# Earlier weights for the third input tile, convolved rows split by token chunk, and a final scale worked out in quarters, in a two-layer hybrid encoder

## The chip, the cores and the metric

The kernel runs on one core of a Trainium2 chip. The metric is the device time of one launch in microseconds (us), as a median over runs. Five engines work side by side, each through its own list of instructions in order: TensorE (PE; its weight loads are shown apart as PEld), VectorE (DVE), ScalarE (ACT), GpSimd (POOL) and SyncE (SP), which issues most of the DMAs.

## The reference

Sixteen learned tokens are put ahead of 1024 input tokens (1040 in all, width 1024), two layers follow, then a norm. Cut to what matters here:

```python
for l in range(DEPTH):                       # DEPTH = 2
    h = h + hybrid_mixer(rmsnorm(h, norm1_w[l]), ...)
    h = h + swiglu(rmsnorm(h, norm2_w[l]), w_gate_up[l], w_down[l])
h = rmsnorm(h, final_norm_w)                 # over the 1024 features of a token
return h[:, N_META:]

def hybrid_mixer(h, ...):
    proj = h @ w_in
    qkv = silu(depthwise_conv_centred(qkv, conv_qkv_w))      # conv over 3 tokens
    o = chunk_gated_delta_rule(forward) + flip(chunk_gated_delta_rule(backward))
    o = o * rsqrt(mean(o * o) + eps) * dn_norm_w * silu(z)
    y_sc = sc_b * depthwise_conv_centred(sc_c * sc_h, sc_conv_w)
    return concatenate([o, y_sc]) @ w_out
```

All of it is float32.

## The kernel before

Features lie on the 128 partitions and tokens along the free axis, so a row tile is 128 features of all 1040 tokens, and the residual is eight such tiles, `hr[0]` to `hr[7]`. A float32 product is made of three matmuls: each operand is split into a high part `hi` (a copy rounded to the matmul's format, made by ACT) and a low part `lo` (the operand less `hi`, made by a subtraction on DVE or POOL); `dense` (L145 to L172) issues hi x hi, hi x lo and lo x hi (L156, L157, L158) for each 128 rows of the contraction, chunk of tokens by chunk of tokens, and then calls the function that empties the PSUM bank. Layer 0 cuts the tokens into three chunks (`FULL`: 348, 346, 346), layer 1's outputs into two of 512 (`TAIL`), and the last down projection of all into 512, 256 and 256 (`FIN`).

**Weights.** `wload` brings 1024 rows of weights in two halves: `wsplit` (L123) issues a DMA on SP to a staging tile `raw` (two of them), ACT makes `whi` (L129), and POOL, or DVE where `lov` says so, makes `wlo` (L130). There are three buffers for `whi` and three for `wlo`. Loads run ahead by way of the dictionary `pre`.

**Input projection.** `seq` gives the order of the first eight tiles, four for the keys and four for the queries. For each: `inproj`, scaling by the token's rstd (L647 for the first tiles, whose products are made before rstd is known), `conv` (one ACT pass, L307, and two DVE passes, L308 and L309), then the call that loads the weights of the next tile, `pre[nxt]`. The first two tiles' weights are loaded ahead of the loop.

**Scan and output projection.** `scan_step(d, c, ...)` handles one chunk of 128 tokens in one direction (L802 to L846): products on PE, DVE's updates of the state, ACT's copies of `vr` (L812 scaled, L814 plain). The short-convolution branch leaves four rows, three of them in DRAM (`yd`), which are read back and split (L899 on ACT; L900 on DVE, row 1's on POOL) into `ys`; the first half of the output projection runs on them under the scan. `finalize` writes the scan's output to `O`, which is split by quarters of the tokens (`hcut`, L928 on ACT, L929 on DVE) for the second half, `out_part`.

**End.** In the last layer the last four feature blocks' products are added to the residual in `FIN` order: per chunk and tile `add_h` (L905, DVE, from PSUM), the square (L187, ACT) and its sum over tiles (L188, DVE), and the scale by the final norm's weight (L1428, ACT). `finish_rstd` (L192) then sums over partitions with a matmul by ones (L196), takes the root on ACT (L197) and the reciprocal over all of the chunk's columns on DVE (L198). DVE and POOL take turns multiplying the tiles (L1432), and SP sends them out in pairs (L1433).

**What sets the order.** The program is written in one order, with priorities: `at_prio` moves a stretch to another place, and `after` adds a wait. The engines' lists are then laid out by a scheduler that simulates the program (`schedule_with_timeline_sim=True`), taking by priority what it believes to be ready. So an edit changes the order through priorities and through the simulated times.

Of the kernel before, what the change touches and what calls it, by code (L numbers as in the profile page):

```python
# [42 lines left out]
def trunk(ctx: ExitStack, tc: tile.TileContext, xT, w_in, w_ba, w_out, w_gu, w_dn,  # L43
# [15 lines left out]
    def row(tag, dt=F32, bufs=1):  # L59
        return sb.tile([128, L], dt, tag=tag, bufs=bufs, name=nm(tag))  # L60
# [218 lines left out]
    for l in range(DEPTH):  # L279
# [357 lines left out]
        for pos, i in enumerate(seq):  # L637
            hh = pos % 4
            if pos == 2:
                gate_weights()  # L640
                evp[0] = base - 60000
            lov[0] = pos > 3
            t = trow()
            late = pos < (2, 1)[l]
            inproj(i, to_row_late(t) if late else to_row(t), pfirst if l == 0 and pos == 1 else None)
            if late:
                tt(out=t, in0=t, in1=rstd, op=ALU.mult)  # L647
            dst = (QT if i < 4 else KTt)[:, hh, :]
            conv(t, dst, P_CV + 3 * i)
            if i >= 4:  # L650
                lengths("k", hh, dst, t)
            if pos == 2:
                g, negG, nGb, negE, gl, bkd = gates()
            nxt = seq[pos + 1] if pos < 7 else 8
            if nxt not in pre:
                pre[nxt] = wload(w_in[l, nxt], KT)
            if pos == 3:
                jobs.append(None)
                jobs.extend([lambda c=c: k_out(c) for c in range(9)])
                jobs2.extend([None, None] + [lambda c=c: chunk_p(c) for c in range(9)])  # L660
# [107 lines left out]
        fin = row(Y[1] + "f")  # L768
        nfin = [0]
        done = set()  # L770

        def v4(t, p=128):
            return t[0:p].rearrange("p (h e) -> p h e", h=4)

        def scan_step(d, c, first, final):
            n = 16 if c == 0 else 128
            s0 = 0 if c == 0 else 16 + 128 * (c - 1)
            base = d * 2048
            V, K, A, Qd = (rec[:, base + 512 * i:base + 512 * i + 512].rearrange("p (h e) -> p h e", h=4) for i in range(4))
            dma(V[0:n].rearrange("p h e -> p (h e)"), vkd[c, 0:n, 0, :])  # L780
            if not final:
                dma(K[0:n].rearrange("p h e -> p (h e)"), vkd[c, 0:n, 1, :])
            if c > 0:
                dma(A.rearrange("p h e -> p (h e)"), aqd[c, d, :, 0, :])
# [12 lines left out]
            if first:  # L797
                r = V
            else:
                ks = b0  # L800
                for h in range(H):
                    mm(ks[0:n, h, :], KTt[:, h, s0:s0 + n], St[d][:, h, :], start=True, stop=True)  # L802
                r = vn
                for h in range(H):
                    stt(out=r[0:n, h, :], in0=ks[0:n, h, :], scalar=negE[0:n, d, c, h:h + 1], in1=V[0:n, h, :], op0=ALU.mult, op1=ALU.add)
            vr = b1
            for h in range(H):
                mm(vr[0:n, h, :], Zs[h], r[0:n, h, :], start=True, stop=True)
            need_o = not (c == 0 and d == 0)
            for h in range(H):  # L810
                if not final:
                    act(out=vs[0:n, h, :], in_=vr[0:n, h, :], func=AF.Copy, scale=bkd[0:n, d, c, h:h + 1])  # L812
            if need_o:
                act(out=vn[0:n], in_=vr[0:n], func=AF.Copy)  # L814
            if not final:
                su = b0
                for h in range(H):
                    mm(su[:, h, :], K[0:n, h, :], vs[0:n, h, :], start=True, stop=True)
            extra = None
            if c == 0 and d == 1:  # L820

                vr2 = b0
                for h in range(H):
                    mm(vr2[0:n, h, :], Z0[0][:, h, :], V[0:n, h, :], start=True, stop=True)
                extra = v4(vv[:, 512:1024])
                act(out=extra[0:n], in_=vr2[0:n], func=AF.Copy)
            if need_o:
                po = b1
                for h in range(H):
                    if not first:  # L830
                        mm(po[0:n, h, :], Qs[h], St[d][:, h, :], start=True, stop=False, skip_group_check=True)
                    mm(po[0:n, h, :], As[h], vn[0:n, h, :], start=first, stop=extra is None, skip_group_check=True)
                    if extra is not None:
                        mm(po[0:n, h, :], at0[0][:, h, :], extra[0:n, h, :], start=False, stop=True, skip_group_check=True)
            if not final:
                for h in range(H):
# [52 lines left out]
        hr = [hb[m // 4][:, m % 4, :] for m in range(KT)]  # L889
        t0 = o0  # L890
        yh = big(X[0][2], F32R)
        ys = []
        for i in range(4):
            t = trow() if i < 2 else hb[1][:, i, :] if i < 3 else y3
            if i < 3:
                dma(t[:, t0:L], yd[i][:, t0:L])
            yl = row(X[1], F32R, 3) if i < 3 else row(X[1] + "f", F32R)
            for (n0, n1) in (chunks if i == 3 else [(t0, L)]):
                act(out=yh[:, i, n0:n1], in_=t[:, n0:n1], func=AF.Copy)  # L899
                (ptt if i == 1 else tt)(out=yl[:, n0:n1], in0=t[:, n0:n1], in1=yh[:, i, n0:n1].bitcast(F32), op=ALU.subtract)  # L900
            ys.append((yh[:, i, :], yl))

        def add_h(m, then=None):
            def f(ps, n0, n1):
# [21 lines left out]
        for (n0, n1) in hcut[0] + hcut[1]:  # L926
            for h in range(H):
                act(out=oh[:, h, n0:n1], in_=O[:, h, n0:n1], func=AF.Copy)  # L928
                tt(out=ol[:, h, n0:n1], in0=O[:, h, n0:n1], in1=oh[:, h, n0:n1].bitcast(F32), op=ALU.subtract)  # L929
        os_ = [(oh[:, h, :], ol[:, h, :]) for h in range(H)]  # L930

        def half(ap, z):
# [485 lines left out]
        if not last:  # L1418
            for m in range(KT):
                then = next_norm(m, x[m], par[:, (l + 1) * P_L + P_N1 + m:(l + 1) * P_L + P_N1 + m + 1], ss)  # L1420
                dense(pre.pop(("dn", m)) if m < 2 else wload(w_dn[l, m, :, 0:NF, :], NF), rest, chunks, add_h(m, then), pwide)
                dma(hd[m], hr[m])
        else:
            for (n0, n1) in FIN:
                for m in range(KT):
                    dense(wds[m], rest, [(n0, n1)], add_h(m), pwide)
                    add_sq(hr[m][:, n0:n1], ss[:, n0:n1], m == 0)
                    act(out=hr[m][:, n0:n1], in_=hr[m][:, n0:n1], func=AF.Copy, scale=par[:, 2 * P_L + m:2 * P_L + m + 1])  # L1428
                finish_rstd(ss, [(n0, n1)])
                for m in range(0, KT, 2):  # L1430
                    for q in (m, m + 1):
                        (tt, ptt)[q % 2](out=hr[q][:, n0:n1], in0=hr[q][:, n0:n1], in1=ss[:, n0:n1], op=ALU.mult)  # L1432
                    dma(out[m:m + 2, :, n0 - 16:n1 - 16].rearrange("m p t -> p m t"), hb[m // 4][:, m % 4:m % 4 + 2, n0:n1])  # L1433
        if not last:
            finish_bc(ss, 0, L, rsd[1])
        hsrc = hd
# [73 lines left out]
```

## Time and profile before

| | us |
|---|---|
| median of 3 runs | 2610.71 |
| lowest and highest | 2609.76, 2611.3 |
| the profiled execution's own time | 2609.5 |
| span of its trace | 2607.7 |

The 1.8 us between the profiled execution's time and its span lie outside the traced instructions. In the profile a row of the timeline gives the start and the duration in us, the engine (a q behind it means its sequencer), the line of the kernel, the operation, what it writes and reads, its shape, how many instructions are merged in the row (x), and in brackets how long the engine had been idle before it and what ended that. `L156` is line 156. Tile names carry no numbers, so `a` and `b` are any tile of those two groups.

### The profile page before, as it was taken

What the parts mean: (1) busy time and instruction counts of PE and PEld (TensorE: products, weight loads), DVE (VectorE), ACT (ScalarE), POOL (GpSimd) and SP (SyncE); (2) the same over time, 40 slices, a digit from 0 to 9 for tenths busy, and PEclk for the clock granted to TensorE, in tenths of its full rate; (3) what the DMA queues carried; (4) which work ended last, traced back from release to release, by engine and by line L of the source; (5) the groups of instructions that cost most, each with busy time, mean ns of one, the idle gap of its engine ahead of it and who ended that gap; (6) DMA issues with size and microseconds to landing.
All of it is one profiled execution on the core that took longest, in us unless ns stands there. A gap on an engine that the chain in (4) does not pass through costs nothing.

```text
span 2607.7 us, 45131 instructions
## 1 busy us (share of the span) xinstructions
PE 2506.3 (96%) x17442; PEld 2291.1 (88%) x17442; DVE 1663.3 (64%) x2481; ACT 1043.8 (40%) x1933; POOL 1113.8 (43%) x838
## 2 busy tenths in 40 slices
PE   8999999999999999999999989999989999999997
PEld 6889999998899999999998978998967778887786
DVE  4678433648766666778455874235687776668756
ACT  5563332435233333444445633224342333333534
POOL 2141212225666666655320202222267766665552
PEclk9999999999999999999999989999999999999998
DMA  3458265524432222664224582545343222238631
GB/s 126 128 181 265 91 207 165 182 67 133 131 98 86 100 81 78 219 211 144 77 95 132 188 275 71 183 158 199 107 126 129 95 93 89 85 107 270 188 98 65
DMA packets 213571, 360.03 MB, mean 138 GB/s; under 512 B 25268, under 2 KB 87676, under 8 KB 213356
## 3 DMA queue, kind: packets, MB, share of 16 engines
q1 hardware_dynamic: 180684, 310.69, 36.6%
q10 hardware_dynamic: 30496, 42.09, 5.2%
q0 software_dynamic: 2176, 4.36, 0.6%
q8 instruction: 137, 2.24, 0.4%
q14 instruction: 78, 0.64, 0.1%
HBM read 266.60 MB, written 90.46 MB: 137 GB/s over the span
## 4 chain that ended last, share of the span: by engine, by line
PE 53%; DVE 9%; DMA 5%; issue 3%; POOL 2%; ACT 1%; SPq 0%; POOLq 0%; DVEq 0%; ACTq 0%
PE pacc L156 4%; PE pacc L158 4%; PE pacc L157 4%; PE pacc L1060 3%; PE pacc L1062 3%; PE pacc L1061 3%; PE pf L1060 2%; PE pb L1060 2%; PE pf L1062 2%; PE pb L1062 2%; PE pb L1061 2%; PE pf L1061 2%; PE pacc L1409 2%; PE pacc L1407 2%; PE pacc L1408 2%
## 5 line engine op out<-in xcount | busy, mean ns | idle before, releaser
L130 POOL TENSOR_TENSOR wlo<-raw,whi 128x512 fp32r<-128x512 f32 x132 | 177.0, 1342 | 789.5 <-ACT whi L129 685.1
L156 PE MATMUL pacc<-a,whi 128*128 128x346 f32 (+1 forms) x808 | 265.2, 331 | 11.7 <-ACT whi L129 8.8
L158 PE MATMUL pacc<-a,wlo 128*128 128x346 f32 (+1 forms) x808 | 264.8, 330 | 2.2 <-DVE wlo L130 1.5
L156 PE MATMUL pacc<-b,whi 128*128 128x346 f32 (+2 forms) x672 | 235.3, 351 | 0.0
L158 PE MATMUL pacc<-b,wlo 128*128 128x346 f32 (+2 forms) x672 | 233.6, 349 | 0.0
L157 PE MATMUL pacc<-a,whi 128*128 128x346 f32 (+1 forms) x688 | 226.4, 329 | 1.8 <-DVE a L900 1.8
L129 ACT ACTIVATE whi<-raw 128x512 fp32r<-128x512 f32 x168 | 105.1, 628 | 243.8 <-PE pacc L157 173.8
L157 PE MATMUL pacc<-b,whi 128*128 128x346 f32 (+2 forms) x580 | 200.6, 347 | 0.5 <-DVE b L900 0.5
L156 PEld LDWEIGHTS pacc<-a,whi 128*128 128x128 f32 x808 | 154.0, 191 | 16.8 <-ACT whi L129 10.4
L1043 POOL TENSOR_TENSOR wlo<-rw,whi 128x512 fp32r<-128x512 f32 x92 | 135.8, 1477 | 72.3 <-ACT whi L1042 70.6
L158 PEld LDWEIGHTS pacc<-a,wlo 128*128 128x128 f32 x808 | 154.4, 191 | 4.1 <-DVE wlo L130 1.9
L156 PEld LDWEIGHTS pacc<-b,whi 128*128 128x128 f32 x672 | 127.6, 190 | 11.0 <-issue 3.1
L157 PEld LDWEIGHTS pacc<-a,whi 128*128 128x128 f32 x688 | 131.4, 191 | 5.8 <-issue 3.4
L158 PEld LDWEIGHTS pacc<-b,wlo 128*128 128x128 f32 x672 | 127.8, 190 | 9.2 <-issue 0.8
L1043 POOL TENSOR_TENSOR a<-rw,a 128x512 fp32r<-128x512 f32 x64 | 105.5, 1650 | 67.3 <-ACT a L1042 67.0
L1043 POOL TENSOR_TENSOR b<-rw,b 128x512 fp32r<-128x512 f32 x64 | 91.9, 1438 | 82.0 <-ACT b L1042 49.2
L157 PEld LDWEIGHTS pacc<-b,whi 128*128 128x128 f32 x580 | 110.2, 190 | 7.8 <-DVE b L900 0.9
L1042 ACT ACTIVATE whi<-rw 128x512 fp32r<-128x512 f32 x92 | 57.8, 630 | 147.3 <-DVE rw L1277 78.2
L1278 DVE TENSOR_TENSOR rw<-raw,rw 128x512 f32<-128x512 f32 x44 | 98.0, 2228 | 1.2
L1273 DVE TENSOR_TENSOR rw<-rw,rw 128x512 f32<-128x512 f32 x44 | 66.3, 1508 | 49.8 <-POOL wlo L1043 30.9
L1043 POOL TENSOR_TENSOR wlo<-raw,whi 128x512 fp32r<-128x512 f32 x50 | 78.5, 1573 | 34.5 <-ACT whi L1042 33.6
L1042 ACT ACTIVATE b<-rw 128x512 fp32r<-128x512 f32 x64 | 40.2, 630 | 119.7 <-PE pacc L1061 32.3
(964 smaller groups left out, 8427.4 us busy)
## 6 DMA issues: line engine op xcount, KB each, us to landing
raw<-in_w_in SPq DMA_DIRECT2D x112, 256.0 KB
raw<-in_w_gu SPq DMA_DIRECT2D x104, 256.0 KB
rw<-in_w_gu SPq DMA_DIRECT2D x88, 256.0 KB
rw<-in_w_dn SPq DMA_DIRECT2D x86, 192.0 KB
rec<-aqd SPq DMA_DIRECT2D x62, 256.0 KB
rec<-vkd SPq DMA_DIRECT2D x61, 256.0 KB
raw<-in_w_out SPq DMA_DIRECT2D x48, 256.0 KB
b<-ad SPq DMA_DIRECT2D x45, 260.0 KB
```

What stands on the lines that cost most here:

```text
L129: act(out=hi, in_=raw[:, 0:kk, :], func=AF.Copy)
L130: (tt if lov[0] else ptt)(out=lo, in0=raw[:, 0:kk, :], in1=hi.bitcast(F32), op=ALU.subtract)
L156: mm(ps[:, :n], wh, xh[:, n0:n1], start=(k == 0), stop=False)
L157: mm(ps[:, :n], wh, xl[:, n0:n1], start=False, stop=False)
L158: mm(ps[:, :n], wl, xh[:, n0:n1], start=False, stop=(k == K - 1))
L1042: act(out=hi, in_=src, func=AF.Copy)
L1043: ptt(out=lo, in0=src, in1=hi.bitcast(F32), op=ALU.subtract)
L1060: mm(ps[:, :CW], w[0][:, k, :], th[:, cs], start=first and k == 0, stop=False, skip_group_check=True)
L1061: mm(ps[:, :CW], w[0][:, k, :], tl[:, cs], start=False, stop=False, skip_group_check=True)
L1062: mm(ps[:, :CW], w[1][:, k, :], th[:, cs], start=False, stop=stop and k == nk - 1, skip_group_check=True)
L1273: tt(out=s1t, in0=A21, in1=A22, op=ALU.add)
L1278: tt(out=A21, in0=A11, in1=A21, op=ALU.subtract)
```

## The change

Four edits, the diff cut to its core:

- In layer 0 the third tile's weights (`seq[2]`) are asked for ahead of the first tile's `conv`, where they were asked for behind the second tile's.
- The split of the four convolved rows goes chunk by chunk, with all four rows of the first chunk ahead of the second chunk; all low parts are made on DVE. In layer 0 the high parts of the later chunks wait for the copy L814 of the backward scan's chunk 1 (`read[1, 1]`).
- Of the low parts of the scan's output (L929), three quarters of the tokens go to POOL, and the first quarter stays on DVE.
- At the end, the sums over partitions go to four strips of 32 partitions, one for each quarter of the chunk's columns, so that root and reciprocal run over a quarter of the columns. Four matmuls by `pick` spread the result to all partitions in PSUM, and ACT copies it to `ss`. The sum over tiles leaves out the last tile, whose squares go to the matmul directly. A chunk's products are handed out one for each tile of the next chunk, most of them to POOL; the last chunk's run at once, six on DVE from PSUM and two on POOL, and their DMAs go one tile each from SP and ACT in turn.

```diff
             dst = (QT if i < 4 else KTt)[:, hh, :]
+            if l == 0 and pos == 0:
+                pre[seq[2]] = wload(w_in[l, seq[2]], KT)
             conv(t, dst, P_CV + 3 * i)
...
             if need_o:
-                act(out=vn[0:n], in_=vr[0:n], func=AF.Copy)
+                read[d, c] = act(out=vn[0:n], in_=vr[0:n], func=AF.Copy)
...
-            yl = row(X[1], F32R, 3) if i < 3 else row(X[1] + "f", F32R)
-            for (n0, n1) in (chunks if i == 3 else [(t0, L)]):
-                act(out=yh[:, i, n0:n1], in_=t[:, n0:n1], func=AF.Copy)
-                (ptt if i == 1 else tt)(out=yl[:, n0:n1], in0=t[:, n0:n1], in1=yh[:, i, n0:n1].bitcast(F32), op=ALU.subtract)
-            ys.append((yh[:, i, :], yl))
+            yt.append(t)
+            ys.append((yh[:, i, :], row(X[1], F32R, 3) if i < 3 else row(X[1] + "f", F32R)))
+        for j, (n0, n1) in enumerate(chunks):
+            for t, (hi, lo) in zip(yt, ys):
+                after(act(out=hi[:, n0:n1], in_=t[:, n0:n1], func=AF.Copy), read.get((1, 1)) if j and not last else None)
+                tt(out=lo[:, n0:n1], in0=t[:, n0:n1], in1=hi[:, n0:n1].bitcast(F32), op=ALU.subtract)
...
-                tt(out=ol[:, h, n0:n1], in0=O[:, h, n0:n1], in1=oh[:, h, n0:n1].bitcast(F32), op=ALU.subtract)
+                (tt if n0 == o0 else ptt)(out=ol[:, h, n0:n1], in0=O[:, h, n0:n1], in1=oh[:, h, n0:n1].bitcast(F32), op=ALU.subtract)
...
+            def last_scale(n0, n1, ps, e):
+                r = c4k("r")[:, 0:e]
+                act(out=r, in_=ps[:, 0:e], func=AF.Sqrt, scale=1.0 / D, bias=cols["eps"])
+                nc.vector.reciprocal(out=r, in_=r)
+                pb = bank("b")
+                for j in range(4):
+                    mm(pb[:, e * j:e * j + e], pick[:, j, :], r, start=True, stop=True)
+                act(out=ss[:, n0:n1], in_=pb[:, 0:n1 - n0], func=AF.Copy)
+                return pb[:, 0:n1 - n0]
+            def scaled(q, n0, n1, mul, by, store):
+                h = hr[q][:, n0:n1]
+                mul(out=h, in0=h, in1=by, op=ALU.mult)
+                store(out[q, :, n0 - 16:n1 - 16], h)
...
             for (n0, n1) in FIN:
+                e = (n1 - n0) // 4
+                def summed(v, first, end):
+                    for j in range(4):
+                        mm(ps[32 * j:32 * j + 32, 0:e], ones[:, 0:32], v[:, e * j:e * j + e], start=first, stop=end, skip_group_check=True)
                 for m in range(KT):
                     dense(wds[m], rest, [(n0, n1)], add_h(m), pwide)
-                    add_sq(hr[m][:, n0:n1], ss[:, n0:n1], m == 0)
-                    act(out=hr[m][:, n0:n1], in_=hr[m][:, n0:n1], func=AF.Copy, scale=par[:, 2 * P_L + m:2 * P_L + m + 1])
-                finish_rstd(ss, [(n0, n1)])
-                for m in range(0, KT, 2):
-                    for q in (m, m + 1):
-                        (tt, ptt)[q % 2](out=hr[q][:, n0:n1], in0=hr[q][:, n0:n1], in1=ss[:, n0:n1], op=ALU.mult)
-                    dma(out[m:m + 2, :, n0 - 16:n1 - 16].rearrange("m p t -> p m t"), hb[m // 4][:, m % 4:m % 4 + 2, n0:n1])
+                    if m < KT - 1:
+                        add_sq(h, sv, m == 0)
+                    else:
+                        summed(sv, True, False)
+                        sq = c4k("sq")[:, 0:n1 - n0]
+                        act(out=sq, in_=h, func=AF.Square)
+                        summed(sq, False, True)
+                    act(out=h, in_=h, func=AF.Copy, scale=par[:, 2 * P_L + m:2 * P_L + m + 1])
+                    if pend:
+                        pend.pop(0)()
+                pb = last_scale(n0, n1, ps, e)
+                if n1 < L:
+                    pend = [lambda q=q, n0=n0, n1=n1, mul=tt if n0 == 16 and q > 5 else ptt: scaled(q, n0, n1, mul, ss[:, n0:n1], dma) for q in range(KT)]
+            for q in range(KT):
+                mul, by = (ptt, sv) if q in (3, 6) else (tt, pb)
+                scaled(q, n0, n1, mul, by, (dma, adma)[q % 2])
```

More of the change, by code (lines that the diff above doesn't have):

```diff
@@ L770, in trunk @@
         done = set()
+        read = {}
         def v4(t, p=128):
@@ L891, in trunk @@
         yh = big(X[0][2], F32R)
-        ys = []
+        ys, yt = [], []
         for i in range(4):
@@ new lines, in scaled @@
+            def scaled(q, n0, n1, mul, by, store):
+                h = hr[q][:, n0:n1]
+                mul(out=h, in0=h, in1=by, op=ALU.mult)
+                store(out[q, :, n0 - 16:n1 - 16], h)
+            pend = []
+            pick = t2k("pick")
+            nc.gpsimd.memset(pick, 0.0)
+            for j in range(4):
+                nc.gpsimd.memset(pick[32 * j:32 * j + 1, j, :], 1.0)
+            for (n0, n1) in FIN:
+                e = (n1 - n0) // 4
+                sv = ss[:, n0:n1]
+                ps = bank("a")
+                def summed(v, first, end):
+                    for j in range(4):
+                        mm(ps[32 * j:32 * j + 32, 0:e], ones[:, 0:32], v[:, e * j:e * j + e], start=first, stop=end, skip_group_check=True)
@@ L1425, in trunk @@
                 for m in range(KT):
+                    h = hr[m][:, n0:n1]
                     dense(wds[m], rest, [(n0, n1)], add_h(m), pwide)
-                    add_sq(hr[m][:, n0:n1], ss[:, n0:n1], m == 0)
-                    act(out=hr[m][:, n0:n1], in_=hr[m][:, n0:n1], func=AF.Copy, scale=par[:, 2 * P_L + m:2 * P_L + m + 1])
-                finish_rstd(ss, [(n0, n1)])
-                for m in range(0, KT, 2):
-                    for q in (m, m + 1):
-                        (tt, ptt)[q % 2](out=hr[q][:, n0:n1], in0=hr[q][:, n0:n1], in1=ss[:, n0:n1], op=ALU.mult)
-                    dma(out[m:m + 2, :, n0 - 16:n1 - 16].rearrange("m p t -> p m t"), hb[m // 4][:, m % 4:m % 4 + 2, n0:n1])
+                    if m < KT - 1:
[5 more added lines that the diff above has]
+                        summed(sq, False, True)
```

## The prediction

> **What bounds the kernel.** I read the page, then TensorE's waits, then the timeline around each edit.
>
> ```profile
> span 2607.7 us, 45131 instructions
> PE 2506.3 (96%) x17442; PEld 2291.1 (88%) x17442; DVE 1663.3 (64%) x2481; ACT 1043.8 (40%) x1933; POOL 1113.8 (43%) x838
> ...
> PE pacc L156 <- ACT whi L129: 8.8, 2, 6.1
> ...
> PE pa L196 <- DVE rstd L188: 5.4, 1, 5.4
> ...
> PE pf L156 <- DVE b L905: 4.8, 2, 2.7
> ```
>
> TensorE bounds the span: idle for 4% of it, about 100 us. An edit gains only where TensorE waits, or after its last product. These rows (who waits for whom, us in total, times, longest) name the places at both ends of the program; the one that the split of the rows aims at shows in the timeline. The profiled execution took 2609.5 us and the median is 2610.71: the sum is made against 2609.5, and 1.2 is added to it.
>
> **Edit 1, the third tile's weights.**
>
> ```profile
> 42.04 0.32 PE L158 MATMUL pacc<-a,wlo 128*128 128x346 f32 x1
> 45.00 0.43 PE L156 MATMUL pacc<-a,whi 128*128 128x348 f32 x1 [2.64 <-ACT whi L129]
> 46.95 0.66 PE L158 MATMUL pacc<-a,wlo 128*128 128x348 f32 x1 [0.73 <-POOL wlo L130]
> ...
> 43.27 1.16 ACT L307 ACTIVATE b<-b,par 128x1040 f32<-128x1040 f32 x1 [8.76 <-DVE b L647]
> 44.33 0.61 ACT L129 ACTIVATE whi<-raw 128x512 fp32r<-128x512 f32 x1
> ...
> 20.71 11.59 SPq L128 DMA_DIRECT2D raw<-in_w_in  x3
> ```
>
> ACT sits idle for 8.76 us, then runs the first tile's convolution pass (43.27), and only behind it, at 44.33, makes the `whi` for which TensorE waits 2.64 us. TensorE ended at 42.36 (42.04 + 0.32), which I read as the moment the buffer that `whi` takes over comes free. With the weights asked for ahead of the convolution, `whi` can start at 42.4 instead of 44.33: 1.9 us. `wlo` follows as much earlier, and of the 0.73 behind it I take off 0.4. The two loads move ahead in SP's list too, but the first loads row shows them issued by 32.3 already, and POOL's subtraction only moves with `whi`. Nothing pays: the convolution waits for DVE's L647 until 43.23, and 42.4 + 0.61 ends before that. Bounds: 0 (ACT's order unchanged) to 3.4 (2.64 + 0.73). A loss has no place here, since ACT was idle. I take **-2.3**.
>
> **Edits 2 and 3, the rows' split.**
>
> ```profile
> 503.00:519.00 16.00, 11.76 (x58) 10.48 (x56) 13.80 (x28) 8.17 (x22) 3.90 (x2) 0.68 0.86 328
> 525.00:541.00 16.00, 16.00 (x106) 12.89 (x105) 6.20 (x14) 3.82 (x13) 1.47 (x2) 1.00 0.11 34
> ...
> 503.99 2.02 ACT L899 ACTIVATE a<-b 128x1040 fp32r<-128x1040 f32 x2
> 506.87 1.24 ACT L899 ACTIVATE a<-b 128x348 fp32r<-128x348 f32 x3
> 508.01 1.11 ACT L812 ACTIVATE vv<-pb,bkd 128x128 f32<-128x128 f32 x4
> ...
> 506.05 4.65 DVE L929 TENSOR_TENSOR o<-b,o 128x260 fp32r<-128x260 f32 x7
> 506.08 2.63 POOL L900 TENSOR_TENSOR a<-b,a 128x1040 fp32r<-128x1040 f32 x1 [0.84 <-ACT a L899]
> 510.62 1.23 DVE L900 TENSOR_TENSOR a<-b,a 128x1040 fp32r<-128x1040 f32 x1
> 511.90 0.66 PE L157 MATMUL pacc<-a,whi 128*128 128x348 f32 x1 [1.84 <-DVE a L900]
> ...
> 523.91 1.29 POOL L130 TENSOR_TENSOR wlo<-raw,whi 128x512 fp32r<-128x512 f32 x1 [15.20 <-ACT pa L865]
> ...
> 1800.00 0.51 PE L157 MATMUL pacc<-b,whi 128*128 128x512 f32 x1 [0.49 <-DVE b L900]
> ```
>
> The first two rows (stretch, length, then busy time and count of PE, PEld, DVE, ACT, POOL, then granted clock) compare two stretches of 16 us of layer 0. In the first, TensorE gets 58 matmuls done at a clock of 0.68, in the second 106 at full clock. At the second's pace 58 take 8.8 us, so the first loses about 7.2 us, idle time and slow clock together: the ceiling of this edit in layer 0.
>
> The cause: ACT splits whole rows from 503.99 on and starts the scan's L812 at 508.01. DVE puts seven subtractions of the scan's output (506.05, 4.65 us) ahead of the first row's `lo`, for which TensorE waits until 511.90. After the edit ACT needs four pieces of 0.41 (1.24 / 3) for the first chunk, so L812 can start near 505.7, 2.3 earlier. DVE, rid of L929, makes the four `lo` pieces at about 0.41 (a third of 1.23) by some 506.5, against 511.84. TensorE then has first-chunk products for two tiles and the scan's products until the later chunks come. Those wait for L814, and no work but the later pieces stands behind that wait, ACT's copies being on the same engine. What stays open is a gap before chunk 1, whose `hi` pieces then run from about 507.4 to 509.1. I leave 2.7 us of the loss standing and take **-4.5**; bounds -7.2 and, if DVE's twelve pieces (4.9 us alone) run at half speed beside POOL, +0.6.
>
> In layer 1 the same wait is only 0.49: **-0.5**, bounds -1 to 0. The twelve subtractions per layer that POOL takes over cost it 12 x 0.66 (1.29 x 260 / 512) alone, which I cost at nothing: the row at 523.91 shows POOL idle for 15.20 us before the next weights. Without that cover they are the third rival.
>
> **Edit 4, the end.**
>
> ```profile
> 2565.99 0.28 PE L156 MATMUL pf<-b,a 128*128 128x256 f32 x1
> 2566.11 0.28 PE L157 MATMUL pf<-b,a 128*128 128x256 f32 x1
> 2583.26 0.39 PE L156 MATMUL pf<-b,a 128*128 128x256 f32 x1 [2.09 <-DVE b L905]
> 2590.76 0.28 PE L158 MATMUL pacc<-b,a3f 128*128 128x256 f32 x1
> 2596.40 1.22 PE L196 MATMUL pa<-rstd,ones 128*128 128x256 f32 x2 [5.36 <-DVE rstd L188]
> ...
> 12.47 0.66 PE L252 MATMUL pb<-sq,ones 128*32 128x260 f32 x8
> 485.90 1.05 PE L802 MATMUL pb<-S,b 128*128 128x128 f32 x8
> ...
> 2572.47 3.35 DVE L198 RECIPROCAL rstd<-rstd 128x512 f32<-128x512 f32 x1 [0.73 <-ACT rstd L197]
> 2576.68 6.19 DVE L1432 TENSOR_TENSOR b<-b,rstd 128x512 f32<-128x512 f32 x4
> 2595.03 0.41 DVE L905 TENSOR_TENSOR b<-pacc,b 128x256 f32<-128x256 f32 x1
> 2598.17 1.75 DVE L198 RECIPROCAL rstd<-rstd 128x256 f32<-128x256 f32 x1 [1.82 <-ACT rstd L197]
> 2599.95 3.01 DVE L1432 TENSOR_TENSOR b<-b,rstd 128x256 f32<-128x256 f32 x4
> ...
> 2575.90 6.42 POOL L1432 TENSOR_TENSOR b<-b,rstd 128x512 f32<-128x512 f32 x4 [40.57 <-DVE rstd L198]
> 2600.00 3.55 POOL L1432 TENSOR_TENSOR b<-b,rstd 128x256 f32<-128x256 f32 x4 [5.17 <-DVE rstd L198]
> ...
> 2576.02 0.74 DVE L905 TENSOR_TENSOR b<-pacc,b 128x256 f32<-128x256 f32 x2
> ...
> 2595.47 0.42 ACT L187 ACTIVATE sq<-b 128x256 f32<-128x256 f32 x1 [2.50 <-DVE b L905]
> 2595.92 0.51 ACT L1428 ACTIVATE b<-b,par 128x256 f32<-128x256 f32 x1
> 2597.66 0.47 ACT L197 ACTIVATE rstd<-pa,epsc 128x256 f32<-128x256 f32 x1 [1.23 <-PE pa L196]
> ```
>
> Up to the last product: the reciprocal (3.35) and the products (6.19) on DVE keep `add_h` waiting, and TensorE with it for 2.09. Both leave DVE, but TensorE gets sums and spreads. Eight sums at 128 columns cost some 0.35 (half of 0.66), twice per chunk; the spread is eight matmuls like L802's, 1.05. For the first two chunks: 0.7 + 1.05 and 0.4 + 0.9, less about 0.7 for the L196 pairs at the products' spacing of 0.12 per 256 columns. That is 2.4 more, so the last product ends 0.3 us later than at 2591.04: **+0.3** (bounds -2 to +3).
>
> After the last product, before: 16.7 us (2591.04 to 2607.7). The last `add_h` starts 4 us late, at 2595.03, behind the previous chunk's products; then follow square, sum, L196, root, reciprocal and four rounds of products. After: `add_h` 0.41, square 0.42, then the scale copy 0.51 ahead of the root while the sum runs beside it. Then the root on 64 columns at 0.3 (below 0.47), and the reciprocal at 0.55: 512 columns take 3.35 and 256 take 1.75, so 6.25 ns a column and 0.15. Then the spread at 1.05 and six products on DVE from PSUM at 0.37, 2.2 in all. With some 0.3 for the hand-overs that is 5.75. POOL's two products, at 0.89 each (3.55 / 4), start half a microsecond after DVE's and end with them. From the last product's end to the end of the span it was 4.1 (2600.00 + 3.55 to 2607.7), which I keep. 5.75 + 4.1 = 9.9, less 16.7: **-6.8**. Bounds: -8.5 (smaller last DMAs land sooner) to -3 (DVE's products slowed to 0.75 as in the row at 2599.95, and a late spread).
>
> Sum: -2.3 - 4.5 - 0.5 + 0.3 - 6.8 = -13.8, so 2595.7 for a profiled execution and **2596.9** for the median.
>
> **Rivals.** *DVE becomes the bound of the last chunks.* POOL now works through chunk 1, and DVE's sums (L188) have two operands in SBUF. L1432's products took 1.55 on DVE beside POOL's (6.19 / 4), while `add_h`, with one operand in PSUM, took 0.37 beside them (2576.02). At 1.55 a sum, one tile costs DVE 1.96, against TensorE's 1.41 (twelve products, 0.1175 apart, 0.12 in the first rows above). Over the six tiles under POOL's long products that is 3.3 us, which puts the result near 2600.2. Against it: a sum has half the columns of those products. The Trainium skill, SBUF — State Buffer, section "SBUF: two separate sides", says that a DVE instruction with two SBUF inputs and a GpSimd one take the shared port pair in turn, each shut out for the whole of the other, which speaks against handing these products to POOL. By that rule the four pairs would have taken the sum of their lone times, and a sum could wait out a whole product of 1.29: 2.1 a tile, and a result near 2601.1. The trace half agrees: the four pairs took 6.97 us from 2575.90, of which POOL was busy for 6.42. Chance 0.14.
>
> *The split does nothing for layer 0.* If L812 and L814 keep their places, chunk 1 cannot start before about 511, the wait moves from `lo` to `hi`, and TensorE idles as before. Result near 2601.4. For it: the later pieces are tied to L814. Against: L812 stood behind six row copies, four microseconds of ACT. Chance 0.14.
>
> *POOL's list delays weights: slower.* In both layers `wlo` of the output projection and the twelve subtractions share POOL's list. At 0.82 each beside DVE (6.42 / 4 x 260 / 512) they are 9.8 us a layer, 19.6 in all. Fully exposed, they give 2616.5. It decides once more than 13.8 of the 19.6 falls on TensorE. Against: the 15.20 us of idle POOL. Chance 0.07.
>
> **Chances.** The forecast gets 0.60, the rivals 0.14, 0.14 and 0.07, and 0.05 goes to orders reshuffled by the scheduler elsewhere that take the gain back, half to no change, half to a loss. A measurement here tells about 0.2%, 5.2 us. The forecast and the first two rivals are faster (0.88); no change 0.04, which takes a little of the third rival; slower 0.08. The range, 2589 to 2606, spans the bounds of terms 2 and 4 without all ends at once: -22 would need every edit at its best, and above 2606 lie the third rival and the reshuffle.
>
> **What would show it.** Right: no wait above 1 us of L156 on `whi` near 42 to 45; L818 near 506 to 507 and some 88 matmuls between 503 and 519; no DVE L929 between 505 and 512; the span's last 16.7 us shrunk to about 10, with reciprocals of about 0.55 and 0.95. Wrong: waits of TensorE on POOL's `wlo` between 505 and 545, on the spread's reciprocal in the last 40 us, or an end more than 12 us after the last product.

## The result and the profile after

| | before | after |
|---|---|---|
| median, us | 2610.24 (6 runs) | 2589.40 (6 runs) |
| lowest and highest | 2605.93, 2614.74 | 2586.91, 2599.71 |
| ratio, 95% interval | | 0.9928, 0.9915 to 0.994 |
| profiled execution, span | 2609.5, 2607.7 | 2589.49, 2587.7 |

The change is faster by 18.8 us, or 0.7%, by the ratio (15.7 to 22.2 us by its interval). The head of the page after (its columns as before):

```profile
span 2587.7 us, 45312 instructions
PE 2504.7 (97%) x17508; PEld 2289.3 (88%) x17508; DVE 1640.2 (63%) x2461; ACT 1047.0 (40%) x1945; POOL 1134.3 (44%) x869
```

TensorE's two largest waits after (us in total, times, longest):

```profile
PE pacc L156 <- ACT whi L129: 8.3, 2, 5.9
PE pf L560 <- DVE a L544: 6.0, 1, 6.0
```

The 5.36 us that TensorE waited on `rstd` L188 near the end, and the 1.84 on the rows' `lo`, are gone from that list. `whi` stands in it almost unchanged (8.8 before), and so does the wait on L544, which the change does not touch (6.1 before). The timeline after, at the beginning (line 156 is still line 156), in layer 0 and at the end:

```profile
45.67 0.66 PE L156 MATMUL pacc<-a,whi 128*128 128x348 f32 x1 [2.40 <-ACT whi L129]
...
43.94 1.16 ACT L307 ACTIVATE b<-b,par 128x1040 f32<-128x1040 f32 x1 [8.52 <-DVE b L647]
45.01 0.61 ACT L129 ACTIVATE whi<-raw 128x512 fp32r<-128x512 f32 x1
...
503.64 1.12 ACT L815 ACTIVATE vv<-pb,bkd 128x128 f32<-128x128 f32 x4
...
503.70 2.04 DVE L905 TENSOR_TENSOR a<-b,a 128x348 fp32r<-128x348 f32 x2
...
503.18 8.13 POOL L933 TENSOR_TENSOR o<-b,o 128x260 fp32r<-128x260 f32 x8
...
2577.43 0.75 DVE L188 TENSOR_TENSOR rstd<-rstd,sq 128x256 f32<-128x256 f32 x1 [0.48 <-ACT sq L187]
2578.10 0.41 DVE L909 TENSOR_TENSOR b<-pacc,b 128x256 f32<-128x256 f32 x1
2579.75 0.55 DVE L1432 RECIPROCAL r<-r 128x64 f32<-128x64 f32 x1 [1.24 <-ACT r L1431]
2580.36 1.10 PE L1435 MATMUL pb<-r,pick 128*128 128x64 f32 x8 [1.02 <-DVE r L1432]
2581.50 0.38 ACT L1436 ACTIVATE rstd<-pb 128x256 f32<-128x256 f32 x1 [1.78 <-PE pb L1435]
2581.92 2.08 DVE L1441 TENSOR_TENSOR b<-b,pb 128x256 f32<-128x256 f32 x6 [1.61 <-ACT rstd L1436]
```

At the beginning nothing has moved: ACT still runs the convolution ahead of `whi`. In layer 0 the scan's copies (L815, which was L812) stand right behind four short row pieces, and DVE makes the rows' low parts without the scan's in between. At the end the last `add_h` (L909) comes straight behind the last product, the reciprocal is 0.55, and DVE's six products take 2.08.

**Where the 20 us went.** Matching each instruction with the same one of the other trace gives the shift of its start; the table has, for stretches of the trace before, how much the median shift of TensorE's instructions changes (the last column by the ends of the spans). All are against the one trace before. The experiments are told below.

| kernel | 0-60 | 490-560 | 1060-1600 | 1870-1910 | 2440-2540 | 2540-end | other | sum |
|---|---|---|---|---|---|---|---|---|
| after | -0.1 | -6.2 | -3.9 | -2.3 | -0.2 | -6.6 | -0.7 | -20.0 |
| after_again (same kernel) | +0.6 | -6.3 | -8.0 | -3.8 | +4.7 | -6.6 | -1.4 | -20.8 |
| edit 1 alone | +0.6 | -1.1 | -5.4 | +0.9 | +5.7 | 0.0 | -0.8 | -0.1 |
| edit 2 alone | +0.7 | -6.1 | -7.2 | -2.5 | +5.5 | 0.0 | -2.9 | -12.5 |
| edit 3 alone | -0.3 | -1.0 | -4.2 | -0.2 | +2.8 | +0.5 | -2.5 | -4.9 |
| edit 4 alone | -0.7 | -0.5 | -3.3 | +0.2 | +3.8 | -6.0 | +0.5 | -6.0 |

Four columns belong to the change: 0 to 60 (edit 1, nothing), 490 to 560 (edit 2 in layer 0), 1870 to 1910 (the end of layer 1's output projection) and the end (edit 4). Two do not: every kernel of the table gains 3 to 8 us between 1060 and 1600, edit 1 alone too, so the trace before was slow there (of the seven kernels that are not in the table one gains as little as 0.5); and between 2440 and 2540 most lose 3 to 6 us, which is the subject of the last experiment. The four columns that belong to the change add to -15.2 for after and -16.1 for its second run. A difference of two spans is good to some 5 us here, a stretch with the change in it to about one.

### The profile page after: what moved, and what is told of

Read it like the earlier page. It is cut to its first block, busy times and chain, and to the rows that moved or that the text cites. A ratio compares the mean times of both kernels' runs of the same rounds, so it can differ in the third digit from the quotient of the medians.

```text
span 2587.7 us, 45312 instructions
## 1 busy us (share of the span) xinstructions
PE 2504.7 (97%) x17508; PEld 2289.3 (88%) x17508; DVE 1640.2 (63%) x2461; ACT 1047.0 (40%) x1945; POOL 1134.3 (44%) x869
```

## The experiments

The first four are the kernel before with one edit each. Each ratio is against the kernel before on the same chip.

**Edit 1 alone.**

```diff
+            if l == 0 and pos == 0:
+                pre[seq[2]] = wload(w_in[l, seq[2]], KT)
             conv(t, dst, P_CV + 3 * i)
```

> The kernel before with edit 1 alone (the third tile's weights asked for ahead of the first convolution). Theory A, formed from the profile after, where TensorE still waits 2.40 us for `whi` near 45 and ACT still runs the convolution pass L307 ahead of it: asking earlier does not move `whi` in ACT's order, so nothing changes: 0.0 us (within +-1), and the wait near 45 stays at 2.4 to 2.6. Rival B, the prediction's step: 1.9 to 2.3 us faster, ACT runs `whi` ahead of L307 and the wait falls below 1.

Measured: ratio 1.0004 (0.999 to 1.0018), which is +1.0 us (-2.6 to +4.7). Theory A holds. The timeline:

```profile
46.28 0.46 PE L156 MATMUL pacc<-a,whi 128*128 128x348 f32 x1 [2.52 <-ACT whi L129]
...
44.55 1.16 ACT L307 ACTIVATE b<-b,par 128x1040 f32<-128x1040 f32 x1 [8.64 <-DVE b L647]
45.62 0.61 ACT L129 ACTIVATE whi<-raw 128x512 fp32r<-128x512 f32 x1
```

The order of instructions on all five engines is the same as before, one for one, so this is in effect a second trace of the kernel before. The edit moves a priority, and that decided nothing; why the scheduler kept its order was not looked into.

**Edit 2 alone.**

```diff
+        for j, (n0, n1) in enumerate(chunks):
+            for t, (hi, lo) in zip(yt, ys):
+                after(act(out=hi[:, n0:n1], in_=t[:, n0:n1], func=AF.Copy), read.get((1, 1)) if j and not last else None)
+                tt(out=lo[:, n0:n1], in0=t[:, n0:n1], in1=hi[:, n0:n1].bitcast(F32), op=ALU.subtract)
```

> The kernel before with edit 2 alone (rows converted chunk by chunk, later pieces behind the scan's copy), the subtractions of L929 left on DVE. In the kernel after the two edits together took 6.2 us out of layer 0 and 2.4 out of layer 1. Theory A (the row pieces carry it, since ACT's six whole-row copies stood ahead of L812): 4 to 6 us faster in layer 0, the scan's L812 starts near 506. Rival B (what carries it is DVE freed of L929's seven subtractions, 4.65 us, ahead of the first `lo`): less than 2 us faster, TensorE still waits over 1 us on DVE's `lo` near 510.

Measured: 0.9962 (0.9946 to 0.9977), -9.9 us; -6.1 in layer 0. Theory A holds, at its edge. The timeline of this kernel on DVE and ACT:

```profile
506.21 0.51 DVE L903 TENSOR_TENSOR a<-b,a 128x348 fp32r<-128x348 f32 x1
506.64 1.43 DVE L931 TENSOR_TENSOR o<-b,o 128x260 fp32r<-128x260 f32 x4
508.00 0.51 DVE L903 TENSOR_TENSOR a<-b,a 128x348 fp32r<-128x348 f32 x1
...
505.73 1.12 ACT L813 ACTIVATE vv<-pb,bkd 128x128 f32<-128x128 f32 x4
```

DVE still makes the scan's low parts (L931), between the row pieces, and TensorE no longer waits for either. L813 runs 2.3 us earlier than L812 before (508.01), and the first row's low part starts at 506.21, where it started at 510.62.

**Edit 3 alone.**

```diff
-                tt(out=ol[:, h, n0:n1], ...)
+                (tt if n0 == o0 else ptt)(out=ol[:, h, n0:n1], ...)
```

> The kernel before with edit 3 alone (L929's subtractions of all but the first half-chunk on POOL), rows still converted whole. Theory A: less than 2 us faster, since L812 still stands behind ACT's row copies. Rival B (DVE freed of L929 is what counts): 4 to 6 us faster in layer 0, the first row's `lo` on DVE ends before 508. A third way: POOL's list delays `wlo` of the output projection, and the kernel is slower by up to 5 us.

Measured: 0.999 (0.9979 to 1.0001), -2.6 us (-5.5 to +0.3), and -1.0 in layer 0, within theory A's bound, but for another reason than A gave. By 510 TensorE runs 6 to 8 us ahead of before, and gives it back:

```profile
515.93 0.42 PE L157 MATMUL pacc<-a,whi 128*128 128x348 f32 x1 [1.91 <-POOL a L900]
...
504.04 9.50 POOL L929 TENSOR_TENSOR o<-b,o 128x260 fp32r<-128x260 f32 x8
513.49 2.39 POOL L900 TENSOR_TENSOR a<-b,a 128x1040 fp32r<-128x1040 f32 x1
```

Row 1's low part is on POOL in the kernel before, and now stands behind eight of the scan's subtractions there, which is a delay by POOL's list, though not of the weights. The next kernel takes that away: edit 3, and row 1's low part on DVE.

```diff
-                (ptt if i == 1 else tt)(out=yl[:, n0:n1], ...)
+                tt(out=yl[:, n0:n1], ...)
```

> The kernel before with edit 3 and the second row's low half moved from POOL to DVE (as edit 2 has it), rows still whole. With edit 3 alone TensorE ran 6 to 8 us ahead by 510 and gave it back by 516: it waited 1.91 us for the second row's low half, which stood on POOL behind the scan's. Theory A (freeing DVE ahead of the first row's `lo` is worth as much as short pieces, and only POOL's list took it back): 4 to 6 us faster than before in layer 0. Rival B (the whole-row copies of ACT ahead of the scan's hold the stage anyway): less than 2 us faster there.

Measured: 0.9966 (0.9955 to 0.9978), -8.9 us; -5.9 in layer 0. Theory A holds, though ACT's list here is that of before: L812 still stands behind all six row copies, 4.0 us after the first of them starts (502.56; 503.99 before).

```profile
506.59 1.11 ACT L812 ACTIVATE vv<-pb,bkd 128x128 f32<-128x128 f32 x4
```

So ACT's long copies do not hold the stage by themselves. There are two ways to the same gain: short pieces, or a DVE without the scan's low parts. Edit 2 without edit 3 has all of it already, so the kernel after without edit 3 should lose nothing:

```diff
-                (tt if n0 == o0 else ptt)(out=ol[:, h, n0:n1], ...)
+                tt(out=ol[:, h, n0:n1], ...)
```

> The kernel after without edit 3: L933's subtractions all on DVE. Theory A (edit 2 alone took 6.1 us out of layer 0, edit 3 adds nothing): within 1.5 us of after. Rival B (edit 3 is needed in company): 2 us slower than after or more.

Measured: 0.9936 (0.9919 to 0.9952), beside 0.9938 for the kernel after on the same chip, and -6.1 in layer 0. Theory A holds: edit 3 earns nothing that these runs can show. The rows above show a price: beside POOL's eight subtractions a piece takes DVE 1.02 in after (2.04 for two at 503.70), against 0.51 in the kernel with edit 2 alone.

**The wait in edit 2.**

```diff
-                after(act(out=hi[:, n0:n1], ...), read.get((1, 1)) if j and not last else None)
+                act(out=hi[:, n0:n1], ...)
```

> The kernel after, without the wait that ties the later row pieces to the scan's last copy (read[1, 1]); L815 and L817 then stand behind twelve row pieces on ACT instead of four. Theory A (in layer 0 what pays is that ACT's scan copies come early; the pieces of the later chunks are 8 of about 0.38 us each): L815 starts about 3 us later, TensorE waits for `vv`, and the kernel is 2 to 4 us slower than after, against before about -15 to -17. Rival B (what pays is that the first chunk's pieces are short, for whatever follows): within 1 us of after.

Measured: 0.9956 (0.994 to 0.9972), -11.5 us. Over 490 to 560 this kernel takes -3.5 against -6.2 for after, and -5.2 to -6.3 for the other kernels with the wait: it is worth some 2 to 3 us there by one trace each, while the intervals of the ratios overlap. A is about right in size. L815 now stands behind all twelve pieces, 4.6 us after the first one, against 1.5 in after (502.11 to 503.64), but A's mechanism does not show: TensorE never waits for `vv`, but some 0.25 at a time for DVE's pieces.

```profile
500.21 0.86 ACT L904 ACTIVATE a<-b 128x348 fp32r<-128x348 f32 x2
504.79 1.11 ACT L815 ACTIVATE vv<-pb,bkd 128x128 f32<-128x128 f32 x4
```

**Edit 4 alone** (its diff stands above as the last edit).

> The kernel before with edit 4 alone (final scale by quarters, products under the next chunk). In the kernel after, from 2550 us on, 6.6 us went. Theory A: the end's gain is its own: 6 to 7 us faster, about 10.3 us from the last product of the dense layer to the end of the span. Rival B: a part of it came from the edits before (buffers or DMAs that stood otherwise): less than 5 us faster.

Measured: 0.9984 (0.9973 to 0.9996), -4.2 us; -6.0 in the trace from 2540 on, and +3.8 just ahead of it. Theory A holds for the end, at its lower bound (10.9 us from the last product to the end of the span); the ratio alone would not tell it from B. The next two are the kernel after with one half of the edit undone. First the products at once:

```diff
-                    pend = [lambda q=q, ...: scaled(q, n0, n1, mul, ss[:, n0:n1], dma) for q in range(KT)]
+                    for q in range(KT):
+                        scaled(q, n0, n1, (tt, ptt)[q % 2], ss[:, n0:n1], dma)
```

> The kernel after, with the products of the first two chunks of the final scale run as soon as their scale is there, by turns on DVE and POOL as before, instead of under the next chunk's products. Theory A (DVE's 6.2 us of products ahead of `add_h` cost TensorE 2.09 us in the kernel before and made the last `add_h` 4 us late): 4 to 5 us slower than after, nearly all of it behind the last dense product. Rival B (the quarter-width reciprocal is what counts): within 1.5 us of after.

Measured: 0.996 (0.9947 to 0.9974); from 2540 on -3.9 against -6.6, so deferring is worth 2.7, between the two, 1.9 of it behind the last product. The last `add_h`s wait behind DVE's products, and TensorE's next work runs slow:

```profile
2575.22 3.63 DVE L1441 TENSOR_TENSOR b<-b,rstd 128x256 f32<-128x256 f32 x4
2578.78 0.41 DVE L909 TENSOR_TENSOR b<-pf,b 128x256 f32<-128x256 f32 x1
...
2581.00 0.32 PE L1457 MATMUL pa<-rstd,ones 128*32 128x64 f32 x8 [2.25 <-DVE rstd L188]
2582.73 1.97 PE L1435 MATMUL pb<-r,pick 128*128 128x64 f32 x8 [1.02 <-DVE r L1432]
```

The same spread took 1.10 in after: the granted clock is 0.50 over it here (2582.70 to 2584.80) and 0.93 there (2580 to 2582). Part of A's 4 to 5 is the reciprocal's, as the next kernel shows. There root and reciprocal run over the full width again:

```diff
-                        mm(ps[32 * j:32 * j + 32, 0:e], ones[:, 0:32], v[:, e * j:e * j + e], ...)
+                    mm(ps[:, 0:n1 - n0], ones, v, start=first, stop=end)
...
-                nc.vector.reciprocal(out=r, in_=r)
+                nc.vector.reciprocal(out=ss[:, n0:n1], in_=ss[:, n0:n1])
```

> The kernel after, with the sum, root and reciprocal over the full width of a chunk (as before), no spread, and the deferred products as in after. Theory A (at the end the quarters save 1.75 - 0.55 of reciprocal and some 0.16 of root and pay 0.9 to 1.05 for the spread and 0.4 for the copy): within 0.7 us of after at the end. Rival B (the quarters carry the end's gain): 2 us slower or more. Either way DVE has 3.35 us of reciprocal in chunk 1, which `add_h` of the next chunk may wait behind: up to 2 us on TensorE near 2565.

Measured: 0.9955 (0.9937 to 0.9973); from 2540 on -3.6 against -6.6. The quarters, with the spread that they need, are worth 3.0, so B is nearer. Of that, 1.5 lies ahead of the last product, in the place of the expectation's last sentence, and 1.4 behind it, where A had 0.7 at most:

```profile
2552.98 3.35 DVE L1431 RECIPROCAL rstd<-rstd 128x512 f32<-128x512 f32 x1 [0.75 <-ACT rstd L1430]
...
2565.78 0.70 PE L1447 MATMUL pa<-rstd,ones 128*128 128x256 f32 x2 [2.11 <-DVE rstd L188]
2576.80 1.75 DVE L1431 RECIPROCAL rstd<-rstd 128x256 f32<-128x256 f32 x1 [1.75 <-ACT rstd L1430]
2578.59 3.16 DVE L1436 TENSOR_TENSOR b<-b,rstd 128x256 f32<-128x256 f32 x6
```

The last row is what theory A left out: without the copy in PSUM the six products read two operands from SBUF beside POOL and take 3.16, not 2.08.

**Edit 1 forced.** The kernel after, where the first convolution's pass on ACT waits for the third tile's `whi`:

```diff
-        act(out=hi, in_=raw[:, 0:kk, :], func=AF.Copy)
+        hiw[0] = act(out=hi, in_=raw[:, 0:kk, :], func=AF.Copy)
...
-            conv(t, dst, P_CV + 3 * i)
+            conv(t, dst, P_CV + 3 * i, hiw[0] if l == 0 and pos == 0 else None)
```

> The kernel after, with the first convolution's pass on ACT (L307 of after) made to wait for the third tile's `whi`, so that edit 1 does in ACT's order what its words say. Theory A (the wait of 2.40 us at 45 is ACT's order): `whi` runs from about 43, the wait falls to about 0.5, and some 1.9 us are gone by 50 us; against after -1.9, if the convolution behind it hides. Rival B (something else, such as the buffer or the convolution's reader, is due as late): the wait moves to another line and the total stays within 0.5 us of after.

Measured: 0.9931 (0.9907 to 0.9954). Theory A holds up to 60 us, and the gain is twice its 1.9: -3.9 there, against -0.1 for after.

```profile
42.35 0.63 ACT L130 ACTIVATE whi<-raw 128x512 fp32r<-128x512 f32 x1 [7.78 <-issue]
43.13 1.17 ACT L308 ACTIVATE b<-b,par 128x1040 f32<-128x1040 f32 x1
...
43.04 0.43 PE L157 MATMUL pacc<-a,whi 128*128 128x348 f32 x1 [0.61 <-ACT whi L130]
```

The waits alone do not make 3.9: before they were 2.64 and 0.73, and here 0.61 is left. TensorE also ran slowly behind them. This is the 5 us from the end of the wait on in the kernel before, with a granted clock of 0.67 and 16 matmuls; the forced kernel has 28 at 1.00 between 43 and 48.

```profile
45.00:50.00 5.00, 4.27 (x16) 3.98 (x17) 2.96 (x2) 1.92 (x2) 1.87 (x1) 0.67 0.15 52
```

The ratio does not show the gain: its interval is too wide for 4 us, and the profiled execution lost 3.8 us between 2440 and 2540, where that of after lost none.

**The stage near 2450, and a version that beats both.** In thirteen traces of the kernels that leave this stage alone TensorE waits there on DVE for 1.4 to 4.75 us, whatever was edited; the kernel after, run again, shows the long form. Its expectation:

> The kernel after, unchanged, beside the three kernels below on the same chip. Theory: 0.992 to 0.994 of before. The wait of TensorE on DVE L1417 near 2450, 1.4 to 4.7 us in ten profiles of kernels that do the same work there, is theory's largest source of scatter in one profile; a second profile of the same kernel may show it at anything between.

Measured: 0.9938 (0.9924 to 0.9951), -16.2 us. TensorE's waits of that run, and DVE and POOL in its timeline:

```profile
PE pa L1411 <- DVE b L1417: 4.7, 1, 4.7
```

```profile
2443.60 1.36 DVE L1154 TENSOR_TENSOR a<-rw,a 128x384 f32<-128x384 f32 x1
2444.88 1.51 DVE L1230 TENSOR_TENSOR P<-a,P 128x512 fp32r<-128x512 f32 x1
2449.12 0.55 DVE L1154 TENSOR_TENSOR a<-rw,a 128x384 f32<-128x384 f32 x1
2449.59 0.68 DVE L1225 TENSOR_TENSOR a<-a,a 128x512 f32<-128x512 f32 x1
...
2444.51 1.34 POOL L1185 TENSOR_TENSOR a<-a,a 128x384 fp32r<-128x384 f32 x1
2445.80 1.45 POOL L1185 TENSOR_TENSOR wlo<-S,whi 128x384 fp32r<-128x384 f32 x1
2447.21 1.44 POOL L1185 TENSOR_TENSOR a<-S,a 128x384 fp32r<-128x384 f32 x1
```

As long as POOL's subtractions run back to back, each of DVE's takes 0.8 us more; when they stop, DVE is at 0.55 and 0.68. The first trace of after has operations of 1.37 to 1.52 on DVE there too, with pauses between POOL's; why one trace has the long wait and another the short one is not shown. The last kernel is the one with edit 1 forced, and eleven of these subtractions on DVE:

```diff
-            ptt(out=lo, in0=r, in1=hi.bitcast(F32), op=ALU.subtract)
+            (tt if last and 46 <= u < 57 else ptt)(out=lo, in0=r, in1=hi.bitcast(F32), op=ALU.subtract)
```

> The kernel after with the third tile's `whi` forced ahead of the convolution (3.4 us gone by 50 us in the run before), and in layer 1 eleven of POOL's subtractions near 2435 to 2456 (L1185, L1186 with the added line) moved to DVE. Theory A (DVE is full there, and each of its SBUF operations takes 1.37 to 1.50 beside a POOL one against 0.54 to 0.68 alone; on DVE the subtraction costs 0.47): DVE's operations near 2440 to 2460 go back to 0.5 to 0.7, the wait on L1417 falls below 1 us, and the kernel is 4 to 6 us faster than after. Rival B (DVE waits there for the loads of `ad`): the wait stays at 1.4 to 4.7, and the kernel is at most 3.4 us faster than after.

Measured: 0.989 (0.9877 to 0.9903), median 2577.23 beside 2588.42 for after and 2605.53 for before on the same chip: -28.7 us against -16.2. DVE's operations are back at their own length, TensorE does not wait on L1418 (L1417 of after), and the granted clock stays at 1.00 (a stretch of 20 us with busy times and counts in the order of the prediction's, then the timeline):

```profile
2430.00:2450.00 20.00, 20.00 (x87) 16.13 (x86) 18.89 (x31) 10.53 (x21) 6.85 (x4) 1.00 0.40 121
```

```profile
2435.62 0.68 DVE L1418 TENSOR_TENSOR b<-pa,b 128x512 f32<-128x512 f32 x1
2436.23 0.54 DVE L1155 TENSOR_TENSOR a<-rw,a 128x384 f32<-128x384 f32 x1
2436.69 0.55 DVE L1186 TENSOR_TENSOR wlo<-a,whi 128x384 fp32r<-128x384 f32 x1
```

Theory A holds, and the gain is twice its 4 to 6. The moved subtractions were not run without the forced wait, so the share of each rests on the traces. Against the second run of after the traces give -4.7 from the first 60 us and -6.5 between 2440 and 2540, together 11.2 of the 12.5. Against the first trace of after, which had the short form of the wait, that stretch gives 1.6. This version is faster than both kernels.

## Why the prediction was right, and where its steps failed

The direction and most of the terms held; the sum of -13.8 was too small against -18.8 (-15.7 to -22.2), and against -16.2 (-12.8 to -19.8) in the second comparison. The measured median of 2589.4 lies only 0.4 inside the fast end of the range of 2589 to 2606. That the sum came as near as it did to the -15.2 of the four stretches is in part luck: the 2.3 us that edit 1 did not give are made up by 2.3 at the end of layer 1's output projection, for which the sum had no term.

- **Edit 1, -2.3: the step failed.** I took ACT's order to follow the priority once the load is asked for earlier. It did not change (edit 1 alone, the order is the same), and the term was 0; my own lower bound named this case, "ACT's order unchanged". The reading of the wait itself was right: forced, `whi` started at 42.35 against the 42.4 that I had read from TensorE's row, and the wait fell to 0.61. The size was off as well, for the term held only the waits: forced, the stretch gave 3.9, with the slow clock behind the wait gone too.
- **Edits 2 and 3 in layer 0, -4.5: right waits, size off.** The trace has -6.2, and about -5.4 after taking off what edits 1 and 4 alone, which do not touch that stage, show in it (-1.1 and -0.5, so the trace before was slow there by about 0.8). The scan's copies came 2.3 earlier in edit 2 alone, as worked out. TensorE got 99 matmuls done between 503 and 519, in a trace that is 2.0 us ahead there, where I had said some 88: the gap before chunk 1, for which I left 2.7 us standing, is mostly not there. Neither half of the argument was needed by itself: edit 2 alone gains 6.1 with L929's work still on DVE, and the kernel with edit 3 and row 1 on DVE gains 5.9 with L812 behind all of ACT's row copies. The stretch after, and the wait before that the prediction's rows leave out, for the scan's copy, ahead of the one on `lo`:

```profile
503.00:519.00 16.00, 14.84 (x99) 13.66 (x99) 15.62 (x31) 7.80 (x26) 9.61 (x10) 1.00 0.76 284
...
508.41 1.65 PE L818 MATMUL pb<-vv,rec 128*128 128x128 f32 x6 [1.52 <-ACT vv L812]
```

- **Layer 1, -0.5: the step was right and not the whole.** The rows' wait gave -0.2 (from 1780 to 1870 the shift goes from -10.1 to -10.3). But between 1870 and 1910 after, its second run and edit 2 alone gain 2.3, 3.8 and 2.5 us: the wait for `add_h` at the end of the output projection, 2.72 before and 0.48 after, is gone or below 0.7 in all kernels with edit 2 and stands at 2.5 to 3.0 with edits 1, 3 or 4 alone. It is gone too in the kernel with edit 3 and row 1's low part on DVE, which differs from edit 3 alone (2.50) in that one line; edit 2 has the same move in it. So what shortens the wait is row 1's low part leaving POOL, or what the scheduler makes of that; the way from there was not followed. In the trace before, an instruction that stands ahead of that `add_h` on DVE waits 1.62 us for the DMA of `hd` (L1001 at 1897.96). I had quoted the wait within the third row of waits of the first fence, where 2.7 is the longest, and costed only its other part, the end's 2.09.

```profile
PE pf L156 <- DVE b L905: 2.7, 1, 2.7
```

That row is the waits between 1880 and 1905 before; after has 0.5 for it.

- **The end, +0.3 and -6.8: right.** The trace gives -0.2 up to the last product (shift -13.4 at 2540; the end of the products went from 2591.04 to 2577.41, 13.6) and -6.4 behind it (16.7 to 10.3). The chain's rows answer to the terms one by one: `add_h` 0.41, root 0.31 for 0.3, reciprocal 0.55 for 0.55, spread 1.10 for 1.05, six products 2.08 for 2.2. From the last product to DVE's last it is 6.6 us (2577.41 to 2584.00) for 5.75, and from there to the end 3.7 for 4.1. Two things I had not listed. The last `add_h` starts 0.7 us behind the last product, as DVE is still at a sum that takes 0.75 beside POOL's products. And DVE's products start only when ACT's copy is done (2581.50 + 0.38, against 2581.92), though they read the PSUM bank itself. The Trainium skill, PSUM — Partial Sum Buffer, section "PSUM bank collisions raise a hardware error", says that two engines must not read the same part of a bank at once, so such accesses are put in order; the rows agree. One sign of being wrong that I had named did show, a wait of 1.02 on the spread's reciprocal (2580.36), but behind the last product, where the sum has the reciprocal as a term; the spreads of the first two chunks have no such wait.
- **The rivals.** *DVE the bound of the last chunks* fell: its sums beside POOL's products did take up to 1.20, in place of 0.42, but TensorE stood still for none of them before the last product.

```profile
2561.23 8.88 POOL L1441 TENSOR_TENSOR b<-b,rstd 128x512 f32<-128x512 f32 x6 [38.73 <-ACT rstd L1436]
...
2569.20 1.20 DVE L188 TENSOR_TENSOR rstd<-rstd,sq 128x256 f32<-128x256 f32 x1
```

  That 1.20 is 0.78 above 0.42, less than one of POOL's products (8.88 / 6 = 1.48), so by the Trainium skill, SBUF — State Buffer, section "SBUF: two separate sides", the sum waited out what was left of one; the trace agrees. *The split does nothing for layer 0* fell with edit 2 alone. *POOL's list delays weights*: no such wait stands near 505 to 545; in edit 3 alone POOL's list did delay a row, and took back what was won.
- **What the sum had no term for** is the scatter of stages that the change does not touch. Edit 1 alone, with the order of before, is 5.8 us ahead of it at 2440 and level at 2540.

## What to carry to other kernels

Before costing an edit that only moves a priority, ask which engine's order it changes; if the order is a scheduler's, an explicit wait does what the priority may not (0 against some 4 us here). When one trace of each kernel is compared, take a kernel with the same order as a control, and read the stage that was edited, not the span. A subtraction moved from DVE to POOL is not free for DVE where DVE is full: moving eleven of another kind off POOL took away a wait that had cost up to 4.75 us.

## What the hardware showed that I had not expected

- **A full DVE beside a busy POOL scatters.** Subtractions of 128x384 with both operands in SBUF take 0.55 on DVE alone and 1.36 beside POOL's. The wait that this gives TensorE went from 1.40 to 4.75 in two traces of one kernel.
- **A long wait is paid up to twice.** In the kernel with edit 1 alone the wait near 2460 is 4.53 instead of 1.64, 2.9 more, and the shift of TensorE changes by 5.7. In the ten traces with a wait of 3.0 or more there, what TensorE loses is 1.5 to 2.1 times what the wait has grown.

```profile
2460.00:2480.00 20.00, 16.12 (x57) 12.86 (x58) 14.34 (x23) 5.08 (x10) 8.06 (x8) 0.83 0.37 102
```

  That is the stretch that holds the last 3.9 us of the wait and what comes behind it: 57 matmuls at a granted clock of 0.83, where before, with its wait of 1.64 in the same stretch, has 80 at 1.00. Waits of 1.4 and 1.6 left the clock at 1.00, those of 3.02 and 3.10 were followed by 0.92 and 0.91 over 20 us, and those of 3.9 to 4.75 gave 0.83 to 0.92. Shorter waits close together lower it too: 2.64 and 0.73 at the beginning of the kernel before (0.67 over 45 to 50), 1.52 and 1.84 in its layer 0 (0.68 over 503 to 519), 2.25 and 1.02 at the end of the kernel with the products at once (0.50 over the spread). The Trainium skill, TensorE: Matmul & The Clock Gate, section "HAM oscillation — how this bites in real kernels", gives idle gaps of some 3.4 us as the point from which the clock falls. The waits of 3.9 us and more agree with it; the shorter ones show that here the clock falls below that point as well.
